# Preparing a projection pair's operands between the products of the pair before it, and sharing its input sums between two engines, in a two-layer hybrid backbone

## The chip, the core and the metric

The kernel runs on one core of a Trainium2 chip. The metric is the device time of one execution in microseconds (us), median over runs. The engines are TensorE (PE, with its weight loads as PEld), VectorE (DVE), ScalarE (ACT), GpSimd (POOL) and SyncE (SP), which here only issues DMAs.

## The reference, cut to what matters

Two layers work on 1024 latent and 256 context tokens of width 1024. A layer normalises and modulates its input to `h`, projects `h` with one matrix `w_in`, gives column groups of the result to four heads (neighbourhood attention, latent attention, a spatial gate, a short convolution), gates them, and projects the joined result back. Only layer 0 updates the context tokens.

```python
hx = modulate(rms_norm(x, norm_g), sh_x, sc_x)
hc = modulate(rms_norm(ctx, norm_g), sh_c, sc_c)
(a_q, a_k, a_v, a_g, b_cq, b_ckv, b_kr, b_g,
 c_u, c_v, c_g, d_b, d_c, d_h, d_g) = jnp.split(hx @ w_in, IN_SPLIT_POINTS, axis=-1)
...
x_new = x + g_x * merge_branches((out_a, out_b, out_c, out_d), (a_g, b_g, c_g, d_g), w_out)
```

The change concerns the product `hx @ w_in` for column groups of 256: `cg`, `dc`, `dh`, `db`, `dg`, `cq`, `ak`, `aq`, `bg`, `ag`.

## The kernel before

`h` is held transposed, as 8 tiles of 128 channels for each of two chunks of 512 latent tokens and one chunk of 256 context tokens, each tile as a high and a low part in a 32-bit matmul format (tag `g`). A plain block (`w_block`, `block_c`) loads 128 columns of weights (512 KB), casts them to a high part on ScalarE (line 362), subtracts it on GpSimd or VectorE for a low part (line 367), and makes three matmuls for each tile: high x high, high x low, low x high.

A pair (`proj2`) does 256 columns for both latent chunks with 7 products in place of 8, in Strassen's manner. `R` holds the right operands: three are tiles of `h` ("11", "21", "22"), four are differences ("1", "2", "3", "4"). For these, `right_parts(i)` adds the high and low parts of four tiles on GpSimd (line 709), `right_sums(i, t)` subtracts the sums on VectorE (line 716) and splits the differences into high and low parts; i runs over 0 to 3. For i of 2 and 3, "3" and "4" live in the tag `o`, whose four buffers hold the token weights of the `av` tiles until those are done. The left operands are four quarters `r` of the weights (four loads of 256 KB, line 736) and combinations of them (lines 740 to 743); `w_op` splits one into a buffer of the tags `wh`, `wl` and `wr` in turn, two buffers each. Operands 0 to 3 are made ahead of the products, 4, 5 and 6 after products 0, 2 and 3. A product is 12 matmuls of 512 columns.

Layer 0 (`half_paired`) makes the first groups as plain blocks, then `value_blocks` (ckv, ten context blocks, the sums, the `av` tiles), then the pairs cq, ak, aq, bg, and ag at the start of the attention stage. Layer 1 (`paired`) has ckv, ak's context blocks, the sums and the `av` tiles, then ten pairs from cg to ag. For bg and ag the tag `wr` is left out of the rotation; it holds two differences instead. Within ag `mla_load` brings attention's operands by DMA, into `g` buffers that the products give back. `kr_rotate` and `kr_transpose` prepare a rotary key between pairs, and `ckv_steps` sends a small power through GpSimd (line 218) on which transposes wait.

The order of instructions on each engine is written at build time by a planner with costs of its own (`schedule_with_timeline_sim=True`); the order of the program is its priority. It may place an instruction ahead of earlier ones that are not ready. `after(a, b)` fixes that a comes behind b on an engine; `pe.chain(True)` does so for all matmuls of a stretch. The tag `x` (20 buffers of 512) holds weights' quarters, sums, gate maps and more.

Of the kernel before, what the change touches and what calls it, by code (L numbers as in the profile page):

```python
# [11 lines left out]
F32R = mybir.dt.float32r  # L12
AF = mybir.ActivationFunctionType
ALU = mybir.AluOpType
# [35 lines left out]
V_NG, V_BM, V_QN, V_KV, V_LN, V_SC, V_FG = 0, 8, 32, 34, 35, 37, 43  # L50
# [46 lines left out]
def backbone(ctx: ExitStack, tc: tile.TileContext, a, yT, dbg=None):  # L97
# [85 lines left out]
    def f(ap):  # L183
        return ap.bitcast(F32)
# [49 lines left out]
    x = {}  # L234
# [191 lines left out]
    def layer(l, H):  # L426
# [263 lines left out]
                spill(scr["kr"][:, :, o:o + n].rearrange("h p n -> p h n"), f(st[64:128]))  # L690


        nop = [0]
        w_tags = ["wh", "wl", "wr"]

        def w_op(raw, lo_eng="pool"):
            t = T(w_tags[nop[0] % len(w_tags)], [2, 512], F32R)
            nop[0] += 1
            split(t[:, 0, :], t[:, 1, :], raw, lo_eng=lo_eng)
            return t.rearrange("p h (k n) -> p h k n", k=4)  # L700

        R = {}

        def right_parts(i):

            t = {}
            for k, (c, kc) in enumerate(((0, i), (1, i), (1, i + 4), (0, i + 4))):
                t[k] = T("x", [512])
                after(pool.tensor_tensor(t[k], f(H[c, kc][:, 0, :]), f(H[c, kc][:, 1, :]), ALU.add), last_split[0])  # L709
            R["11", i], R["21", i], R["22", i] = H[0, i], H[0, i + 4], H[1, i + 4]  # L710
            return t

# [13 lines left out]
                              skip_group_check=True)  # L726
                    n += 1

        def proj2(base, evac, mid={}, raw="x"):

            r = {}
            for j in range(2):
                t = T("st", [2, 512]) if raw == "st" else None
                for k in range(2):
                    r[j, k] = T("x", [512]) if t is None else t[:, k]
                    sp.dma_start(r[j, k], a["wtb"][l, BLOCKS.index(f"{base}{j}")][:, k * 512:(k + 1) * 512])
            qt = T("wr", [2, 512]) if "wr" not in w_tags else None
            q = [T("x", [512]) if qt is None else qt[:, k] for k in range(2)]
            a11, a12 = w_op(r[0, 0]), w_op(r[0, 1])
            dve.tensor_tensor(q[1], r[0, 0], r[1, 0], ALU.subtract)  # L740
            dve.tensor_tensor(r[1, 0], r[1, 0], r[1, 1], ALU.add)
            dve.tensor_tensor(q[0], r[1, 0], r[0, 0], ALU.subtract)
            dve.tensor_tensor(r[0, 1], r[0, 1], q[0], ALU.subtract)
            ops = {0: a11, 1: a12, 2: w_op(q[0], "dve"), 3: w_op(r[1, 0])}
            later = {0: (4, q[1], "dve"), 2: (5, r[0, 1], "dve"), 3: (6, r[1, 1], "pool")}
            x_, y_, z_ = PS("b", [512]), None, None

            def step(n, p, name, first=True):
                for fn in mid.get(n, []):
                    fn()  # L750
                product(p, ops[n], name, first)
                if n in later:
                    k, src, eng = later[n]
                    ops[k] = w_op(src, eng)

            def kept_copy(eng, p):
                t = T("tmp", [512])
                (eng.copy if eng is act else eng.tensor_copy)(t, p)
                return t

            step(0, x_, "11")
            m1 = kept_copy(act, x_)
            y_ = PS("b", [512])
            step(1, y_, "21")
            dve.tensor_tensor(m1, y_, m1, ALU.add)
            evac(0, m1, 0)
            step(2, x_, "2", False)
            u2 = kept_copy(act, x_)
            z_ = PS("b", [512])
            step(3, z_, "1")  # L770
            z5 = kept_copy(dve, z_)
            step(4, x_, "3", False)
            dve.tensor_tensor(z5, x_, z5, ALU.add)
            evac(1, z5, 1)
            step(5, z_, "22", False)
            dve.tensor_tensor(u2, z_, u2, ALU.add)
            evac(1, u2, 0)
            step(6, x_, "4", False)
            evac(0, x_, 1)

        def block_c(name, c, evac, **k):

# [39 lines left out]
                proj(f"db{j}", all_chunks, mulb)  # L822
                proj(f"dg{j}", all_chunks, lambda c, p: gate(c, p, fc))

        def value_blocks(ctx_first):

            wav = w_tok(a["wav"][l], 288, ("o", "o"), ("o", "o"))
            pe.chain(True)
            late = []

            def ckv_block(c, hi, lo):
                p = PS("b", [CHUNKS[c][1]])
                mm3(p, [(hi[:, kc, :], lo[:, kc, :], hap(c, kc, 0), hap(c, kc, 1)) for kc in range(KC)])
                late.append(ckv_steps(c, p))

            def on():
                for fn in [fns.pop(0) for fns in late if fns]:
                    fn()

            w = w_block(a["wtb"][l, BLOCKS.index("ckv0")])  # L840
            ckv_block(2, *w)
            ckv_block(1, *w)
            ckv_block(0, *w)
            for n, (name, fn) in enumerate(ctx_first):
                block_c(name, 2, fn, lo_eng=("dve", "pool")[n % 3 == 2])
# [12 lines left out]
            pe.chain(False)  # L858
            av_windows()

        def half_paired():
            first_groups()
            while fillers:
                fillers.pop(0)()
            park((4, 5, 6, 7))
            evacs = {"cq": cq_evac, "ak": k_evac, "aq": lambda c, p, j: q_evac(c, p, j, 0.125),
                     "bg": lambda c, p, j: act.activation(map_(2 + j, c), p, AF.Silu),
                     "ag": lambda c, p, j: act.activation(map_(j, c), p, AF.Silu)}
            value_blocks([(f"{n}{j}", lambda c, p, n=n, j=j: evacs[n](c, p, j)) for n in evacs for j in range(2)])
            proj2("cq", evacs["cq"])  # L870
            kr = kr_rotate()
            proj2("ak", k_evac)
            kr_transpose(*kr)
            proj2("aq", evacs["aq"])
            cq_stats()
            w_tags.remove("wr")
            proj2("bg", evacs["bg"])

        def paired():
            wav = w_tok(a["wav"][l], 288, ("o", "o"), ("o", "o"))  # L880
# [19 lines left out]
                fns.pop(0)()  # L900
            av_tile(8, wav)
            late[-1].pop()()
            parts.append(right_parts(1))
            for t in (9, 4):
                av_tile(t, wav)
            cv_gate(1)
# [7 lines left out]
                av_tile(t, wav)  # L914
            pe.chain(False)
            av_windows()
            proj2("cg", lambda c, p, j: gate(c, p, 4 + j))
            park((4, 5))
            proj2("dc", lambda c, p, j: act.copy(map_(6 + j, c), p))
            kr = kr_rotate()  # L920
            z = {}

            def conv_in(c, p, j):
                z[j, c] = T("x", [512])
                dve.tensor_tensor(z[j, c], p, map_(6 + j, c), ALU.mult)

            proj2("dh", conv_in)
            kr_transpose(*kr)
            for j in range(2):
                w = [v[:, V_SC + 3 * j + i:V_SC + 3 * j + i + 1] for i in range(3)]  # L930
                for c in range(2):
                    m = map_(6 + j, c)
                    act.activation(m, z[j, c], AF.Copy, scale=w[1])
                    for d, s_, k in ((m[:, 1:], z[j, c][:, :511], 0), (m[:, :511], z[j, c][:, 1:], 2),
                                     (m[:, 0:1], z[j, 0][:, 511:], 0) if c else (m[:, 511:], z[j, 1][:, 0:1], 2)):
                        dve.scalar_tensor_tensor(d, s_, w[k], d, ALU.mult, ALU.add)

            def mulb(c, p, j):
                m = map_(6 + j, c)
                dve.tensor_tensor(m, p, m, ALU.mult)  # L940

            proj2("db", mulb)
            proj2("dg", lambda c, p, j: gate(c, p, 6 + j))
            park((6, 7))
            proj2("cq", cq_evac)
            proj2("ak", k_evac)
            proj2("aq", lambda c, p, j: q_evac(c, p, j, 0.125))
            cq_stats()
            w_tags.remove("wr")
            proj2("bg", lambda c, p, j: act.activation(map_(2 + j, c), p, AF.Silu))  # L950

        ph = Phase("prj", ("o",))
        if last:
            paired()
        else:
            half_paired()


        ck, cq, up = {}, {}, {}
# [744 lines left out]
```

## Time and profile before

| | us |
|---|---|
| median of three runs | 1507.06 |
| the runs | 1506.96, 1512.91, 1507.06 |
| profiled execution | 1513.53 |
| its span, first to last instruction | 1511.7 |
| TensorE busy in it | 1402.0 (93%) |
| mean granted TensorE clock in it | 0.976 |

The granted clock is a share of the full 2.4 GHz. A busy TensorE is not TensorE at its peak: matmuls are pipelined, and at a lower clock the same matmuls are busy for longer.

### The profile page before, as it was taken

What the parts mean: (1) busy time and instruction counts of PE and PEld (TensorE: products, weight loads), DVE (VectorE), ACT (ScalarE), POOL (GpSimd) and SP (SyncE); (2) the same over time, 40 slices, a digit from 0 to 9 for tenths busy, and PEclk for the clock granted to TensorE, in tenths of its full rate; (3) what the DMA queues carried; (4) which work ended last, traced back from release to release, by engine and by line L of the source; (5) the groups of instructions that cost most, each with busy time, mean ns of one, the idle gap of its engine ahead of it and who ended that gap; (6) DMA issues with size and microseconds to landing.
All of it is one profiled execution on the core that took longest, in us unless ns stands there. A gap on an engine that the chain in (4) does not pass through costs nothing.

```text
span 1511.7 us, 23317 instructions
## 1 busy us (share of the span) xinstructions
PE 1402.0 (93%) x8784; PEld 1173.9 (78%) x8784; DVE 947.7 (63%) x2007; ACT 646.0 (43%) x1438; POOL 552.1 (37%) x441
## 2 busy tenths in 40 slices
PE   4999999896999999999999989799999899999997
PEld 3788888794777777778888889577787677778887
DVE  5867887365446776764555646747453677665564
ACT  5511111333344765654433422433343566655543
POOL 2154343266324000365712174734434001065651
PEclk9999999998899999999999999899999999999998
DMA  9414345514449000786333111340339403285331
GB/s 355 171 61 158 127 154 182 164 44 149 139 153 195 1 22 1 171 175 185 119 126 126 43 45 67 129 119 31 133 133 218 88 1 78 81 178 150 95 130 67
DMA packets 91312, 180.10 MB, mean 119 GB/s; under 512 B 9280, under 2 KB 35904, under 8 KB 91072
## 3 DMA queue, kind: packets, MB, share of 16 engines
q1 hardware_dynamic: 74176, 150.30, 30.5%
q0 software_dynamic: 15936, 27.27, 9.6%
q8 instruction: 69, 1.13, 0.3%
q10 hardware_dynamic: 1088, 1.05, 0.2%
q14 instruction: 43, 0.35, 0.1%
HBM read 144.77 MB, written 38.01 MB: 121 GB/s over the span
## 4 chain that ended last, share of the span: by engine, by line
PE 75%; DVE 6%; issue 5%; DMA 5%; POOL 4%; ACT 3%; SPq 1%; DVEq 0%; ACTq 0%; POOLq 0%
PE psb L173 59%; PE psv L173 7%; PE pst L176 7%; PE pst L173 1%; DMA x<-in_wtb 1%; DMA wr<-in_wtb 1%; POOL s L218 1%; POOL x L709 1%; DVE x L716 1%; DVE s L1106 1%; DMA g<-scr_cq 1%; POOL wl L367 1%; DVE pt L995 1%; ACT g L1253 1%; DMA wr<-in_wav 1%
## 5 line engine op out<-in xcount | busy, mean ns | idle before, releaser
L173 PE MATMUL psb<-g,wh 128*128 128x512 f32 (+1 forms) x1886 | 505.2, 370 | 26.2 <-ACT wh L362 22.0
L173 PEld LDWEIGHTS psb<-g,wh 128*128 128x128 f32 x1886 | 341.1, 193 | 92.7 <-ACT wh L362 24.6
L173 PE MATMUL psb<-g,wl 128*128 128x512 f32 (+1 forms) x1144 | 369.4, 375 | 11.9 <-ACT wl L362 7.3
L173 PEld LDWEIGHTS psb<-g,wl 128*128 128x128 f32 x1144 | 219.7, 193 | 55.2 <-ACT wl L362 9.4
L173 PE MATMUL psb<-g,st 128*128 128x512 f32 (+1 forms) x600 | 160.1, 383 | 10.3 <-ACT wl L1123 3.8
L1106 DVE TENSOR_REDUCE s<-psb 128x1 f32<-128x512 f32 (+1 forms) x200 | 117.3, 590 | 64.6 <-PE psb L173 62.7
L367 POOL TENSOR_TENSOR wl<-wr,wh 128x1024 fp32r<-128x1024 f32 (+1 forms) x38 | 92.9, 2445 | 137.3 <-ACT wh L362 136.1
L173 PE MATMUL psb<-g,g 128*128 128x256 f32 (+1 forms) x784 | 129.0, 305 | 1.8 <-ACT g L1123 0.8
L173 PEld LDWEIGHTS psb<-g,st 128*128 128x128 f32 x600 | 95.6, 192 | 34.8 <-issue 6.5
L173 PE MATMUL psv<-pt,g 128*64 128x256 f32 (+1 forms) x1312 | 119.4, 331 | 0.6 <-ACT pt L997 0.5
L997 ACT COPY pt<-pst 128x512 f32<-128x512 f32 x116 | 67.9, 585 | 111.5 <-PE pst L176 110.4
L173 PEld LDWEIGHTS psb<-g,g 128*128 128x128 f32 x784 | 105.3, 191 | 8.6 <-issue 2.9
L173 PEld LDWEIGHTS psv<-pt,g 128*64 128x64 f32 x1312 | 79.3, 137 | 32.5 <-issue 8.5
L173 PE MATMUL psb<-g,wr 128*128 128x512 f32 (+1 forms) x490 | 97.9, 346 | 5.1 <-ACT wr L362 2.6
L340 DVE CUSTOM_DVE_ANT_0 tmp<-g,x 128x512 f32<-128x512 f32 x112 | 92.5, 876 | 13.4 <-POOL x L490 11.2
L173 PEld LDWEIGHTS psb<-g,wr 128*128 128x128 f32 x490 | 77.5, 190 | 17.9 <-ACT wr L362 3.7
L176 PE MATMUL pst<-ident,g 128*128 128x128 f32 x448 | 79.1, 278 | 11.3 <-ACT g L1253 6.4
L364 POOL TENSOR_SCALAR wh<-wr 128x1024 fp32r<-128x1024 f32 x16 | 44.3, 2772 | 113.0 <-PE pst L176 53.2
L995 DVE COPY pt<-pst 128x512 f32<-128x512 f32 x116 | 79.1, 683 | 6.7 <-PE pst L176 6.1
L1439 DVE SCALAR_TENSOR_TENSOR x<-psb,modG,x 128x512 f32<-128x512 f32 (+1 forms) x48 | 29.5, 615 | 85.1 <-PE psb L173 45.6
L362 ACT CAST wh<-wr 128x1024 fp32r<-128x1024 f32 (+1 forms) x41 | 40.3, 986 | 91.0 <-PE psb L173 58.5
L176 PEld LDWEIGHTS pst<-ident,g 128*128 128x128 f32 x448 | 54.0, 140 | 28.0 <-ACT g L1253 8.3
(249 smaller groups left out, 2387.4 us busy)
## 6 DMA issues: line engine op xcount, KB each, us to landing
g<-in_wmod SPq DMA_DIRECT2D x48, 512.0 KB, 4.7
x<-in_wtb SPq DMA_DIRECT2D x60, 256.0 KB, 4.1
wr<-in_wtb SPq DMA_DIRECT2D x28, 512.0 KB, 4.1
wr<-in_wout SPq DMA_DIRECT2D x27, 512.0 KB, 3.8
st<-in_nab SPq DMA_DIRECT2D x24, 384.0 KB, 3.3
x<-in_xT SPq DMA_DIRECT2D x32, 256.0 KB, 5.8
g<-scr_q POOLq DMA_DIRECT2D x32, 256.0 KB, 7.2
x<-x SPq DMA_DIRECT2D x24, 256.0 KB, 2.5
```

The source lines that it names most:

```text
L173: return self._next(nc.tensor.matmul(*p, **k))
L176: return self._next(nc.tensor.transpose(*p, **k))
L218: pool.tensor_tensor(r0, v, mhalf[:, :n], ALU.pow)
L340: dve.tensor_tensor_reduce(junk, w[:, hf * 512:hf * 512 + 512], crow[cond, hf], 1.0, 0.0, ALU.mult, ALU.add, part[:, i, cond, hf:hf + 1])
L362: act.copy(hi, raw)
L364: pool.tensor_scalar(hi, raw, 1.0, None, ALU.mult)
L367: m = (pool if lo_eng == "pool" else dve).tensor_tensor(lo, raw, f(hi), ALU.subtract)
L709: after(pool.tensor_tensor(t[k], f(H[c, kc][:, 0, :]), f(H[c, kc][:, 1, :]), ALU.add), last_split[0])
L995: dve.tensor_copy(dst, src)
L997: act.copy(dst, src)
L1106: dve.reduce_max(st["mx"][:, i:i + 1], s_, AX.X)
L1439: dve.scalar_tensor_tensor(xa, p, mod[l]["G"][:, fb, cond:cond + 1], xa, ALU.mult, ALU.add)
```

## The change

`proj2` becomes a class `Pair` whose steps can be called one by one. `load` issues the four loads, `sums` makes three differences, `op` splits one operand (the fourth difference is made with operand 5), `prep` does the loads, the sums and operands 0 to 3. `run(nxt)` makes the seven products and, after products 1, 3, 4, 5 and 6, calls the next pair's `load`, `sums` and `op`. The first pair of each layer is prepared by `prep` ahead of the sums' `right_parts`; in layer 1 `right_parts(0)` and `(1)` stand together behind it. `right_parts` gives its first and third addition to VectorE. All pairs but ag use three operand tags; differences live in `x` buffers for all.

```diff
             for k, (c, kc) in enumerate(((0, i), (1, i), (1, i + 4), (0, i + 4))):
                 t[k] = T("x", [512])
-                after(pool.tensor_tensor(t[k], f(H[c, kc][:, 0, :]), f(H[c, kc][:, 1, :]), ALU.add), last_split[0])
+                m = (pool if k % 2 else dve).tensor_tensor(t[k], f(H[c, kc][:, 0, :]), f(H[c, kc][:, 1, :]), ALU.add)
+                after(m, last_split[0] if k % 2 else gated.get(1, gated[0]))
...
-        def proj2(base, evac, mid={}, raw="x"):
...
+        class Pair:
+
+            count = 0
+
+            def __init__(self, base, evac, mid={}, tags=("wh", "wl", "wr")):
+                self.base, self.evac, self.mid, self.tags, self.ops = base, evac, mid, tags, {}
+
+            def load(self):
+                self.r = r = {}
+                for j in range(2):
+                    for k in range(2):
+                        r[j, k] = T("x", [512])
+                        sp.dma_start(r[j, k], a["wtb"][l, BLOCKS.index(f"{self.base}{j}")][:, k * 512:(k + 1) * 512])
+
+            def sums(self):
+                r = self.r
+                self.q = q = [T("x", [512]) for _ in range(2)]
+                dve.tensor_tensor(q[1], r[0, 0], r[1, 0], ALU.subtract)
+                dve.tensor_tensor(r[1, 0], r[1, 0], r[1, 1], ALU.add)
+                dve.tensor_tensor(q[0], r[1, 0], r[0, 0], ALU.subtract)
+
+            def op(self, n):
+                r, q = self.r, self.q
+                if n == 5:
+                    dve.tensor_tensor(r[0, 1], r[0, 1], q[0], ALU.subtract)
+                src = (r[0, 0], r[0, 1], q[0], r[1, 0], q[1], r[0, 1], r[1, 1])[n]
+                t = T(self.tags[Pair.count % len(self.tags)], [2, 512], F32R)
+                Pair.count += 1
+                split(t[:, 0, :], t[:, 1, :], src, lo_eng="dve" if n in (2, 4, 5) else "pool")
+                self.ops[n] = t.rearrange("p h (k n) -> p h k n", k=4)
+
+            def prep(self):
+                self.load()
+                self.sums()
+                for n in range(4):
+                    self.op(n)
+
+            def run(self, nxt=None):
+                evac = self.evac
+                todo = {0: [lambda: self.op(4)], 2: [lambda: self.op(5)], 3: [lambda: self.op(6)]}
+                if nxt:
+                    todo[1] = [nxt.load]
+                    todo[3].append(nxt.sums)
+                    todo[4] = [lambda: nxt.op(0)]
+                    todo[5] = [lambda: nxt.op(1)]
+                    todo[6] = [lambda: nxt.op(2), lambda: nxt.op(3)]
...
+                def step(n, p, name, first=True):
+                    for fn in self.mid.get(n, []):
+                        fn()
+                    product(p, self.ops.pop(n), name, first)
+                    for fn in todo.get(n, []):
+                        fn()
...
-        def value_blocks(ctx_first):
+        def value_blocks(ctx_first, first):
...
             for t in (8, 9):
                 av_tile(t, wav)
+            first.prep()
             parts = [right_parts(0), right_parts(1)]
...
-            proj2("cq", evacs["cq"])
+            pairs = [Pair(n, evacs[n]) for n in ("cq", "ak", "aq", "bg")] + [ag_pair()]
...
+            pairs[0].run(pairs[1])
             kr = kr_rotate()
-            proj2("ak", k_evac)
+            pairs[1].run(pairs[2])
             kr_transpose(*kr)
-            proj2("aq", evacs["aq"])
+            pairs[2].run(pairs[3])
             cq_stats()
-            w_tags.remove("wr")
-            proj2("bg", evacs["bg"])
+            pairs[3].run(pairs[4])
...
+        def ag_pair():
+            return Pair("ag", lambda c, p, j: act.activation(map_(j, c), p, AF.Silu), {1: [lambda: mla_load()], 6: [lambda: mla_keys(0)]},
+                     ("wh", "wl"))
...
             late[-1].pop()()
-            parts.append(right_parts(1))
...
+            pairs["cg"].prep()
+            parts = [right_parts(0), right_parts(1)]
             for t in (9, 4):
                 av_tile(t, wav)
...
+            for name, nxt in zip(names, names[1:]):
+                pairs[name].run(pairs[nxt])
+                for fn in behind_pair.get(name, []):
+                    fn()
...
-        proj2("ag", lambda c, p, j: act.activation(map_(j, c), p, AF.Silu), {1: [mla_load], 6: [lambda: mla_keys(0)]})
+        ag_run.run()
```

`behind_pair` holds what stood between the pairs before (`park`, `kr_rotate`, `kr_transpose`, the convolution, `cq_stats`), at the same places.

## Rows read from the trace of the kernel before

**Rows 1.** Page, head and part 1: busy time, share of the span, instructions of each engine.

```profile
span 1511.7 us, 23317 instructions
...
PE 1402.0 (93%) x8784; PEld 1173.9 (78%) x8784; DVE 947.7 (63%) x2007; ACT 646.0 (43%) x1438; POOL 552.1 (37%) x441
```

**Rows 2.** Windows of layer 0; columns: length, busy time (instructions) of each engine, granted clock, DMA.

```profile
341.00:372.80 31.80, 22.74 (x84) 17.27 (x84) 20.14 (x21) 11.55 (x20) 18.11 (x14) 0.84 0.37 130
372.80:384.40 11.60, 4.16 (x13) 2.73 (x12) 3.91 (x6) 3.55 (x6) 9.62 (x18) 0.66 0.83 271
384.40:434.40 50.00, 49.99 (x216) 40.90 (x217) 27.48 (x41) 21.29 (x37) 14.57 (x10) 0.94 0.37 123
434.40:450.60 16.20, 13.72 (x57) 10.21 (x56) 4.96 (x12) 5.16 (x10) 2.66 (x4) 1.00 0.49 165
```

**Rows 3.** The same columns for stretches of layer 1.

```profile
899.20:904.00 4.80, 0.24 (x2) 0.00 (x0) 2.26 (x8) 0.60 (x1) 3.41 (x2) 0.81 0.00 0
948.50:1001.80 53.30, 42.40 (x168) 32.59 (x168) 30.85 (x33) 19.11 (x33) 34.65 (x35) 0.90 0.39 124
1001.80:1028.00 26.20, 22.41 (x100) 17.19 (x99) 17.28 (x25) 11.15 (x19) 6.54 (x6) 1.00 0.36 107
1028.00:1148.40 120.40, 119.67 (x516) 96.64 (x516) 70.53 (x96) 45.05 (x79) 43.94 (x30) 0.99 0.36 124
1148.40:1173.60 25.20, 23.36 (x94) 18.28 (x93) 10.53 (x17) 12.19 (x22) 18.12 (x22) 0.93 1.02 198
```

**Rows 4.** Timeline of layer 0, start of the first pair.

```profile
339.97 2.50 POOL L367 TENSOR_TENSOR o<-x,o 128x512 fp32r<-128x512 f32 x2 [9.82 <-ACT o L362]
...
342.43 5.39 POOL L709 TENSOR_TENSOR x<-g 128x512 f32<-128x512 f32 x4
...
347.78 1.71 POOL L367 TENSOR_TENSOR wh<-x,wh 128x512 fp32r<-128x512 f32 x1
...
350.75 5.46 PE L173 MATMUL psb<-g,wh 128*128 128x512 f32 x12 [7.26 <-ACT wh L362]
```

**Rows 5.** Timeline of layer 0, between the first and the second pair.

```profile
375.16 10.66 SPq L736 DMA_DIRECT2D x<-in_wtb  x10
...
376.63 3.33 POOL L675 TENSOR_TENSOR x<-tmp 128x128 f32<-128x128 f32 x8
...
378.24 1.22 PE L173 MATMUL psb<-g,wl 128*128 128x512 f32 x2 [5.43 <-ACT wl L362]
```

**Rows 6.** Timeline of layer 1, GpSimd's additions and TensorE behind them.

```profile
886.01 12.07 POOL L709 TENSOR_TENSOR x<-g 128x512 f32<-128x512 f32 x8
...
904.03 0.69 PE L176 MATMUL pst<-ident,s 128*128 128x128 f32 x2 [4.59 <-DVE s L223]
```

**Rows 7.** Lines 709 and 716, both layers: instructions, ns min/median/max, first and last start.

```profile
L709 POOL TENSOR_TENSOR x<-g x32: 1259/1292/2353, 302.4 to 954.8; 128x512 f32<-128x512 f32 x32
...
L716 DVE TENSOR_TENSOR x<-x,x x32: 675/1602/1790, 306.0 to 965.6; 128x512 f32<-128x512 f32 x32
```

**Rows 8.** Chain of work in order of time, end of layer 1's last pair.

```profile
1157.25 7.61 DMA g<-scr_ck
...
1165.37 10.54 DMA g<-scr_cq
```

**Rows 9.** Windows, layer 0's context blocks, columns as in rows 2.

```profile
268.50:308.80 40.30, 33.25 (x249) 31.82 (x249) 16.68 (x31) 14.36 (x25) 17.58 (x11) 0.92 0.51 164
```

**Rows 10.** Groups of instructions in the context blocks' stretch.

```profile
L362 ACT CAST wh<-wr 128x1024 fp32r<-128x1024 f32 x8 | 8.4, 1046 | 18.3 <-DMA wr<-in_wtb 9.5 <-PE psb L173 8.8
```

**Rows 11.** Page, part 6: DMA issues, KB each, us to landing.

```profile
wr<-in_wtb SPq DMA_DIRECT2D x28, 512.0 KB, 4.1
...
x<-in_wtb SPq DMA_DIRECT2D x60, 256.0 KB, 4.1
```

**Rows 12.** Timeline of SyncE's queue in layer 0, ahead of the context blocks.

```profile
213.91 0.33 SPq L395 DMA_DIRECT2D wr<-in_wav  x1
...
231.64 0.33 SPq L373 DMA_DIRECT2D wr<-in_wtb  x1
```

More of the change, by code (lines that the diff above doesn't have):

```diff
@@ L690, in kr_transpose @@
                 spill(scr["kr"][:, :, o:o + n].rearrange("h p n -> p h n"), f(st[64:128]))
[L693 to L700, printed above, removed]
         R = {}
@@ L727, in product @@
                     n += 1
-        def proj2(base, evac, mid={}, raw="x"):
[L731 to L779, printed above, removed]
@@ new lines, in layer, with kept_copy @@
+        class Pair:
[43 more added lines that the diff above has]
+                        fn()
+                def kept_copy(eng, p):
+                    t = T("tmp", [512])
+                    (eng.copy if eng is act else eng.tensor_copy)(t, p)
+                    return t
+                x_ = PS("b", [512])
+                step(0, x_, "11")
+                m1 = kept_copy(act, x_)
+                y_ = PS("b", [512])
+                step(1, y_, "21")
+                dve.tensor_tensor(m1, y_, m1, ALU.add)
+                evac(0, m1, 0)
+                step(2, x_, "2", False)
+                u2 = kept_copy(act, x_)
+                z_ = PS("b", [512])
+                step(3, z_, "1")
+                z5 = kept_copy(dve, z_)
+                step(4, x_, "3", False)
+                dve.tensor_tensor(z5, x_, z5, ALU.add)
+                evac(1, z5, 1)
+                step(5, z_, "22", False)
+                dve.tensor_tensor(u2, z_, u2, ALU.add)
+                evac(1, u2, 0)
+                step(6, x_, "4", False)
+                evac(0, x_, 1)
@@ L902, in paired @@
             late[-1].pop()()
-            parts.append(right_parts(1))
+            pairs = {"cg": Pair("cg", lambda c, p, j: gate(c, p, 4 + j)),
+                     "dc": Pair("dc", lambda c, p, j: act.copy(map_(6 + j, c), p)), "dh": Pair("dh", conv_in),
+                     "db": Pair("db", mulb), "dg": Pair("dg", lambda c, p, j: gate(c, p, 6 + j)),
+                     "cq": Pair("cq", cq_evac), "ak": Pair("ak", k_evac),
+                     "aq": Pair("aq", lambda c, p, j: q_evac(c, p, j, 0.125)),
+                     "bg": Pair("bg", lambda c, p, j: act.activation(map_(2 + j, c), p, AF.Silu)), "ag": ag_pair()}
+            pairs["cg"].prep()
+            parts = [right_parts(0), right_parts(1)]
             for t in (9, 4):
@@ L916, in paired @@
             av_windows()
[L917 to L950, printed above, removed]
+            names = list(pairs)
+            behind_pair = {"cg": [lambda: park((4, 5))], "dc": [lambda: kr.extend(kr_rotate())],
+                           "dh": [lambda: kr_transpose(*kr), conv], "dg": [lambda: park((6, 7))], "aq": [cq_stats]}
+            kr = []
+            for name, nxt in zip(names, names[1:]):
+                pairs[name].run(pairs[nxt])
+                for fn in behind_pair.get(name, []):
+                    fn()
+            return pairs["ag"]
         ph = Phase("prj", ("o",))
[L953 to L956, printed above, removed]
+        ag_run = paired() if last else half_paired()
         ck, cq, up = {}, {}, {}
```

19 lines of the change are left out of this document (18 added, 1 removed).

## The prediction

> **What bounds the kernel now.** I read part 1 of the page first. TensorE is busy for 1402 us of a span of 1511.7 us [rows 1], so only its idle time and its time at a low clock can be won. Next come the windows, which say where those lie in the two projection stages. In layer 0 TensorE works 22.74 of 31.80 us in the first pair, at a granted clock of 0.84, and 4.16 of 11.60 us between the first pair and the second, at 0.66 [rows 2]. From 384.4 on it is full. Layer 1 looks the same: 0.24 of 4.80 us before the last ckv steps, 42.40 of 53.30 us in the first two pairs, and then 119.67 of 120.40 us [rows 3]. The reader is to see that the middle pairs already run without gaps, so that this change can win only at the ends of the stages.
>
> Then the timeline shows what is waited for. At the first pair of layer 0 GpSimd splits the last "o" tiles, runs four additions of right_parts for 5.39 us, and only at 347.78 makes the low half of the pair's first operand; TensorE's next run of products starts at 350.75 after 7.26 us of waiting [rows 4]. Before the second pair SyncE issues its loads from 375.16, behind the spills of the first, and TensorE has waited 5.43 us when operand 0 comes [rows 5]. In layer 1 eight additions hold GpSimd for 12.07 us, and TensorE waits 4.59 us at 904.03 for a chain that needed GpSimd in that time [rows 6].
>
> **The price of a pair.** The covered stretch 1028.0 to 1148.4 holds 516 TensorE instructions in 120.40 us, 0.233 us each [rows 3]. A pair has 7 products of 12 matmuls, 84 x 0.233 = 19.6 us. The change adds and removes no matmul, so every stretch is priced as its TensorE instructions x 0.233.
>
> **Preparing ahead (Pair.prep, load, sums, op).** Layer 0 [rows 2]:
> - first pair, 31.80 - 19.6 = 12.2 us above price: its four loads, three sums and operands 0 to 3 move to before the av tiles that fill TensorE;
> - up to the second pair, 11.60 - 13 x 0.233 = 8.6 us: its loads move from behind the spills of cq to behind product 1;
> - 384.4 to 434.4, 50.00 - 216 x 0.233 = -0.3, so nothing;
> - bg to ag, 16.20 - 57 x 0.233 = 2.9 us: bg keeps the third operand tag and the differences leave it.
>
> That is 23.7 us. Layer 1 [rows 3]:
> - first two pairs, 53.30 - 168 x 0.233 = 14.2 us;
> - third pair, 26.20 - 100 x 0.233 = 2.9 us: the fourth pair's loads no longer stand behind kr's spills;
> - 1028.0 to 1148.4, 0;
> - last pair, 25.20 - 94 x 0.233 = 3.3 us.
>
> That is 20.4 us, and 44.1 us for both layers, if nothing is late next.
>
> **Halved additions.** Moving two of four additions to VectorE takes 2 x 1.29 = 2.6 us off GpSimd per call [rows 7]. Behind the last "o" split this leaves 2.6 instead of 5.39 us before GpSimd is free [rows 4], so the differences for products 2, 3, 4 and 6 come about when TensorE wants them, 5.6 us after the start (two products). This is part of the 12.2 and 14.2 us and not counted again. In layer 1 the additions also move behind the prepared operands, out of the way of the chain at 904.03: another 4.80 - 2 x 0.233 = 4.3 us [rows 3, 6]. The ceiling is 44.1 + 4.3 = 48.4 us.
>
> VectorE pays: an addition or subtraction of this shape takes it 0.675 us at best and 1.60 in the median, while GpSimd's holds at 1.29 [rows 7]. I read this as VectorE being held while GpSimd works. Eight calls x 2 additions x 0.675 to 1.60 us is 11 to 26 us of VectorE time, nearly all of it while av tiles occupy TensorE. Cover gone, only the two calls for the last index would show, at up to 3.2 us each.
>
> The Trainium skill (SBUF — State Buffer, "SBUF: two separate sides") speaks against this edit: it says that GpSimd and a VectorE instruction with two SBUF inputs exclude each other from one port pair for a whole instruction. By that rule four additions take 2 x (1.29 + 0.675) = 3.9 us instead of about 3.2 in parallel. The sum would be some 1.4 us worse; the rows agree for VectorE, whose median is drawn out, and not for GpSimd.
>
> **What is late next.** I take off:
> - First pairs: VectorE is busy 20.14 us and GpSimd 18.11 us in the 31.80 us of layer 0's first pair [rows 2]. Of these some 4 us of sums and low halves leave VectorE for earlier, and about as much comes in for the next pair. 20 us of VectorE work in 19.6 us cannot fit without gaps. Nothing to 5 us per layer; I take 3, so 6.
> - kr_rotate: its eight copies alone take GpSimd 3.33 us [rows 5], in a gap that vanishes. They now stand between low halves of operands. Nothing to 3.3 us per layer; I take 1 in all, since an operand is due two products after its cast.
> - The prepared work itself: no row shows loads, casts and sums of a pair among context blocks or av tiles. From below, nothing: that stretch's DMA share is 0.51 and TensorE idles 7 of 40.3 us anyway [rows 9]. From above, one load, 4.1 us [rows 11], on the path in each layer, 8.2 us. I take 2, nearer to nothing, because four loads lie among free queue time.
> - The end: ag's keys and queries arrive by transfers of 7.61 and 10.54 us, one after the other [rows 8], and the first can start only when the first products have given their buffers back. 2.8 + 7.6 + 10.5 = 20.9 us from the pair's start stands against 19.6 us of products, so 1 to 2 us come back. I take 1.
>
> The sum of these is 10 us (0 to 23.5: 10, 3.3, 8.2 and 2). 48.4 - 10 = 38.4 us.
>
> The sum was made against the profiled execution, 1513.5 us (span 1511.7 and 1.8 around it); that gives 1475. It is 6.5 us above the median of the runs, 1507.1, and I found no stretch to put that on. I take the saving over unchanged: 1507.1 - 38.4 = 1468.7, say **1469 us**.
>
> **The clock.** The first two windows of rows 2 were granted 0.84 and 0.66, a mixture of 2.4 GHz and of 1.2 GHz after TensorE's waits; pricing them at 0.233 us already counts that back. The Trainium skill (TensorE: Matmul & The Clock Gate, "What's actually happening") calls the low state the default, released by activity; the rows agree, and no extra term follows.
>
> **Rivals.**
> 1. *VectorE and GpSimd become the bound of the first pairs.* For: 20.14 and 18.11 us busy in layer 0's first pair, 30.85 and 34.65 us in layer 1's first two [rows 2, 3]. Against: part of it moves ahead. If the first pairs kept half of what they have above price, (12.2 + 14.2)/2 = 13.2 us, and the other three costs were at their upper ends, 13.5, the saving is 48.4 - 26.7 = 21.7: about 1485 us. Chance 0.18.
> 2. *Written order changes little.* The order on each engine is a planner's, and before the change it already issued ten loads in a row, two pairs ahead [rows 5]. It may place the new program's loads as late as before. Then only the additions count: 4.3 us, and 2.6 + 2.6 us at the starts, about 1497 us. Against: the late loads stood behind spills that come first in the program, and this order is now reversed. Chance 0.08.
> 3. *Slower: the prepared operands sit in the context blocks' buffers.* Operands 0 to 3 need four of the six wh, wl and wr buffers, from prep to the pair. If they got them before layer 0's last context blocks had theirs, these would run one at a time: load 4.1, cast 1.05 and products 33.25/10 = 3.3 us are at least 8.4 instead of 40.3/10 = 4.0 us a block [rows 9 to 11], 4.4 us more. With all ten it is 44 us, which eats the whole gain of 38; with these costs on top, 1513 us. It decides from nine blocks on. Against: the loads of wav, written between two other users of wr, went out between them, at 213.91 and before the 231.64 of the next weight block [rows 12], so a tag's buffers are handed out in program order, and prep stands behind the last context block. Chance 0.05.
>
> **How the numbers follow.** My forecast (saving 28 to 50 us, 1457 to 1479) has 0.69, the rivals 0.18, 0.08 and 0.05. The range 1453 to 1490 takes in the forecast with the costs at nothing, 1507.1 - 48.4 = 1459 and some room below for gaps that I priced as covered, and most of rival 1; it leaves out rivals 2 and 3 and the tails, about 0.18. About 0.5%, 7.5 us, is what a measurement of this kernel can tell from no change. The forecast and the first two rivals lie below that, but for a little of the second: faster 0.92, same 0.03, slower 0.05.
>
> **What would show it.** Right: TensorE in layer 0 goes from the last av tile into 24 matmuls of products 0 and 1 without a wait; the first load of ak leaves SyncE before the first spill of cq; no wait near 904 in layer 1; the windows of the first pairs shrink from 31.8 to some 22 us and from 53.3 to some 43, at a clock near 1. Wrong: new waits of TensorE on low halves by VectorE or GpSimd in the first pairs (rival 1), loads still behind spills (rival 2), context blocks longer than the 40.3 us of rows 9 (rival 3), or a longer wait on the last transfers.

## The result and the profile after

The changed kernel takes **1470.65 us** (median of four runs, 1469.06 to 1471.41) against 1507.19 us before (four runs), a ratio of 0.9747 with a 95% interval of 0.9722 to 0.9772 (the two medians alone give 0.9758). The forecast was 1469, the range 1453 to 1490. The total was right by luck: two of its terms were wrong, in opposite directions.

**What both texts ahead left out.** In layer 1 the changed program still calls `right_parts(0)` behind `cv_gate(0)`, and calls it again behind `prep`. The first call's four sums are never read. So there are 36 additions, not 32; the prediction counted eight calls.

The page of the changed kernel, head and part 1, beside [rows 1]:

```profile
span 1467.3 us, 23300 instructions
...
PE 1380.6 (94%) x8784; PEld 1161.1 (79%) x8784; DVE 960.9 (65%) x2025; ACT 643.0 (44%) x1438; POOL 538.3 (37%) x427
```

TensorE has the same 8784 matmuls in a span 44.4 us shorter. Cut at events of TensorE, the profiled executions divide as follows (differences of start and end times in the timelines, us; for the experiments too, which come below). "to av end" is the span's start to layer 0's last av tile, "pairs 0" from there to the last product of ag, "to gate" from there to the first matmul of layer 1's `cv_gate(0)`, "ckv, av" from there to layer 1's last av tile, "pairs 1" to its last product of ag, "rest" to the end.

| kernel | to av end | pairs 0 | to gate | ckv, av | pairs 1 | rest |
|---|---|---|---|---|---|---|
| before | 341.0 | 132.2 | 432.9 | 42.2 | 225.2 | 338.1 |
| after | 339.1 | 108.5 | 427.6 | 55.4 | 202.9 | 333.8 |
| one call | 341.0 | 106.9 | 428.0 | 52.3 | 202.9 | 334.8 |
| all on GpSimd | 336.2 | 110.9 | 428.1 | 55.5 | 207.8 | 339.2 |
| first pairs late | 338.9 | 111.8 | 428.7 | 51.0 | 211.4 | 334.5 |
| nothing between products | 339.2 | 121.9 | 430.1 | 56.2 | 215.3 | 335.2 |
| halving alone | 340.6 | 129.9 | 429.1 | 47.9 | 221.3 | 335.9 |
| VectorE's behind ckv | 341.7 | 108.4 | 427.6 | 48.1 | 202.8 | 334.2 |
| both behind ckv | 339.4 | 106.9 | 428.2 | 48.7 | 202.8 | 335.5 |
| GpSimd alone, behind ckv | 337.5 | 112.9 | 427.6 | 47.7 | 207.1 | 334.8 |
| tiles ahead | 338.1 | 108.4 | 427.6 | 45.3 | 202.5 | 333.7 |
| tiles ahead, both behind | 341.1 | 106.8 | 427.6 | 41.0 | 208.5 | 334.1 |

Before to after: 1.9 + 23.7 + 5.3 - 13.2 + 22.3 + 4.3 = 44.3 us. The medians lie 36.5 us apart, because the profiled execution of before was 6.3 us above its median and that of after 1.6 us below.

Layer 0's pairs, in windows with the columns of [rows 2]:

```profile
339.10:358.70 19.60, 16.28 (x67) 12.36 (x67) 14.22 (x19) 8.62 (x17) 13.42 (x10) 0.98 0.63 215
358.70:378.30 19.60, 19.32 (x79) 15.37 (x78) 10.50 (x12) 7.85 (x14) 14.41 (x21) 0.93 0.50 164
378.30:397.90 19.60, 19.60 (x95) 16.14 (x95) 12.39 (x19) 7.80 (x14) 3.88 (x3) 1.00 0.62 209
397.90:447.60 49.70, 49.70 (x225) 40.64 (x224) 27.18 (x43) 22.99 (x41) 27.22 (x30) 1.00 0.88 226
```

A window of 19.6 us is as long as the price of a pair, and the first one holds 67 of the first pair's 84 matmuls. The whole pair goes from 339.10 to 363.92, where the second pair's first matmul starts: 24.82 us, with TensorE busy for 21.50, VectorE for 17.24 and GpSimd for 15.82 us, at a clock of 0.93. For the same 84 matmuls the first line of [rows 2] has 31.80 us, 22.74, 20.14, 18.11 and 0.84. The timeline there, beside [rows 4]:

```profile
338.93 2.94 PE L173 MATMUL psb<-g,wh 128*128 128x512 f32 x12
...
341.71 2.96 PE L173 MATMUL psb<-g,wl 128*128 128x512 f32 x12
342.48 2.54 POOL L700 TENSOR_TENSOR x<-g 128x512 f32<-128x512 f32 x2
...
351.37 2.37 PE L173 MATMUL psb<-g,wl 128*128 128x512 f32 x9 [1.16 <-POOL wl L367]
...
354.81 0.69 DVE L740 TENSOR_TENSOR x<-x,x 128x512 f32<-128x512 f32 x1
355.59 0.62 ACT L362 CAST wh<-x 128x512 fp32r<-128x512 f32 x1 [4.74 <-DVE x L740]
356.11 0.58 ACT L777 COPY tmp<-psb 128x512 f32<-128x512 f32 x1
...
356.74 2.02 PE L173 MATMUL psb<-g,wl 128*128 128x512 f32 x6 [2.16 <-ACT tmp L777]
```

Products 0 and 1 start behind the last av tile without a wait, where 7.26 us were waited before; GpSimd's two additions (line 700 is now that of `right_parts`) still run beside product 1. One wait of 1.16 us and two on an eviction, a copy out of a matmul buffer (2.4 us together), are what is left in these pairs. The longer of the two, 2.16 us, comes from VectorE: ScalarE's copy (line 777) stands behind a cast that waited 4.74 us for VectorE's sums of the second pair (line 740). SyncE's queue shows why the second pair no longer waits, beside [rows 5]:

```profile
339.77 0.89 SPq L733 DMA_DIRECT2D x<-in_wtb  x2
...
341.24 0.88 SPq L733 DMA_DIRECT2D x<-in_wtb  x2
...
354.20 13.59 SPq L560 DMA_DIRECT2D scr_cq<-st  x3
```

ak's four loads leave at 339.8 to 342.1, ahead of the first spill of cq at 354.20; before, the first left at 373.81 and the next from 375.16, behind the spills.

In layer 1 TensorE's waits from the spatial gate to ag's end are these (line waited for, releaser: us in total, times, longest):

```profile
PE pst L176 <- DVE s L223: 13.1, 1, 13.1
PE psb L173 <- ACT tmp L777: 1.6, 3, 0.8
PE psb L173 <- ACT g L362: 0.9, 1, 0.9
```

The first of them is new. The timeline around it:

```profile
884.07 0.15 DVE L598 TENSOR_SCALAR s<-pst 128x4 f32<-128x4 f32 x1
...
884.34 1.46 POOL L218 TENSOR_TENSOR s<-s,mhalf 128x4 f32<-128x4 f32 x1
...
887.77 1.74 DVE L740 TENSOR_TENSOR x<-x,x 128x512 f32<-128x512 f32 x1
888.93 6.78 POOL L700 TENSOR_TENSOR x<-g 128x512 f32<-128x512 f32 x4
889.44 1.75 DVE L700 TENSOR_TENSOR x<-g 128x512 f32<-128x512 f32 x1
891.11 1.22 DVE L220 SCALAR_TENSOR_TENSOR s<-s,s 128x4 f32<-128x4 f32 x1
892.25 4.01 DVE L700 TENSOR_TENSOR x<-g 128x512 f32<-128x512 f32 x3
...
897.56 0.15 DVE L223 SCALAR_TENSOR_TENSOR s<-s,s 128x4 f32<-128x4 f32 x1
...
897.85 1.08 PE L176 MATMUL pst<-ident,s 128*128 128x128 f32 x4 [13.11 <-DVE s L223]
```

The last ckv step's power on GpSimd is done at 885.80. Its three small scalings on VectorE (lines 220 to 223) end at 897.71, 11.9 us later, because sums of the pair's quarters, low halves and four additions stand between them. The four transposes wait for them, and av tiles stand behind the transposes. The windows (columns as above) show the clock there:

```profile
880.00:885.00 5.00, 4.74 (x38) 4.51 (x37) 5.00 (x8) 2.17 (x5) 5.00 (x4) 1.00 0.45 153
885.00:890.00 5.00, 0.00 (x0) 0.00 (x0) 5.00 (x5) 1.87 (x4) 5.00 (x4) 0.69 0.41 149
890.00:895.00 5.00, 0.00 (x0) 0.00 (x0) 5.00 (x5) 0.22 (x1) 5.00 (x4) 0.50 0.00 0
895.00:900.00 5.00, 2.15 (x10) 2.18 (x11) 4.02 (x8) 0.88 (x2) 0.71 (x1) 0.50 0.00 0
```

TensorE idles for 13 us and comes back at 0.50, 1.2 GHz: its four transposes take 1.08 us, against 0.60 us for four like them at 880.06.

### The profile page after: what moved, and what is told of

The parts are those of the page before. It is cut to its first block, busy times and chain, and to the rows that moved or that the text cites. A ratio compares the mean times of both kernels' runs of the same rounds, so it can differ in the third digit from the quotient of the medians.

```text
span 1467.3 us, 23300 instructions
## 1 busy us (share of the span) xinstructions
PE 1380.6 (94%) x8784; PEld 1161.1 (79%) x8784; DVE 960.9 (65%) x2025; ACT 643.0 (44%) x1438; POOL 538.3 (37%) x427
## 5 line engine op out<-in xcount | busy, mean ns | idle before, releaser
L173 PE MATMUL psb<-g,wh 128*128 128x512 f32 (+1 forms) x1862 | 489.4, 363 | 4.3 <-ACT x L502 1.4
L173 PEld LDWEIGHTS psb<-g,wh 128*128 128x128 f32 x1862 | 330.7, 189 | 65.2 <-ACT x L502 1.9
L173 PE MATMUL psb<-g,wl 128*128 128x512 f32 (+1 forms) x1114 | 356.3, 369 | 5.7 <-ACT tmp L777 3.1
L173 PEld LDWEIGHTS psb<-g,wl 128*128 128x128 f32 x1114 | 210.1, 189 | 44.7 <-ACT tmp L777 4.4
L173 PE MATMUL psb<-g,wr 128*128 128x512 f32 (+1 forms) x544 | 110.4, 348 | 1.1 <-ACT g L362 0.9
L173 PEld LDWEIGHTS psb<-g,wr 128*128 128x128 f32 x544 | 87.7, 189 | 15.1 <-ACT g L362 1.3
L364 POOL TENSOR_SCALAR wh<-wr 128x1024 fp32r<-128x1024 f32 x16 | 44.3, 2772 | 113.0 <-PE pst L176 52.9
```

The source lines that it names most:

```text
L173: return self._next(nc.tensor.matmul(*p, **k))
L364: pool.tensor_scalar(hi, raw, 1.0, None, ALU.mult)
```

## The experiments

The theory at the start was that VectorE's share of the additions holds the scalings of the last ckv step. The rival was that the planner puts the additions, on whichever engine, and the prepared work ahead of that step. A second question was how the gain divides among preparing the first pairs early, preparing between products, and halving. All edits are to the changed kernel unless said otherwise. The times of before in the three sets of runs were 1508.77, 1510.19 and 1510.79 us; ratios are to before in the same set. Beside the changed kernel before took 1507.19 us, so up to 3.6 us of a difference between medians of two sets can be that of the sets.

**One call.** The unread first call is taken out.

```diff
             cv_gate(0)
-            parts = [right_parts(0)]
```

> Changed kernel (1470.7 us) without the first of the two calls of right_parts(0) in layer 1, whose four sums nothing reads. Theory A (VectorE's queue: additions and prepared sums stand inside the ckv scaling chain, and TensorE waits 13.1 us for it near 885 us): two VectorE additions of about 1.75 us and two of GpSimd leave that stretch, the wait falls by 3 to 5 us, 1466 to 1468. Theory B (the wait is set by GpSimd's power, lines 218, behind its own additions): GpSimd had 2.5 us of them ahead of the power, the wait falls by at most 2.5 us, 1468 to 1471.

Measured: 1466.40 us, 0.9718 (0.9695 to 0.9741). The wait fell from 13.1 to 8.7 us, as in the first case. The time is 4.3 us lower than after's, but the two intervals overlap; it is the wait that shows the gain. In the timeline of this run both engines are in the way:

```profile
884.80 4.52 DVE L700 TENSOR_TENSOR x<-g 128x512 f32<-128x512 f32 x3
...
885.39 6.71 POOL L700 TENSOR_TENSOR x<-g 128x512 f32<-128x512 f32 x4
...
889.57 0.14 DVE L598 TENSOR_SCALAR s<-pst 128x4 f32<-128x4 f32 x1
...
892.07 1.46 POOL L218 TENSOR_TENSOR s<-s,mhalf 128x4 f32<-128x4 f32 x1
```

Three additions on VectorE stand ahead of the instruction that makes the power's input (line 598), which ends at 889.71. Four on GpSimd then hold the power itself until 892.07. The scalings follow it at once, at 893.56.

**All on GpSimd.** The additions are not halved; the unread call stays.

```diff
-                m = (pool if k % 2 else dve).tensor_tensor(t[k], ...)
-                after(m, last_split[0] if k % 2 else gated.get(1, gated[0]))
+                m = pool.tensor_tensor(t[k], ...)
+                after(m, last_split[0])
```

> Changed kernel with all additions of right_parts on GpSimd again, all behind the last split (the doubled call stays). Theory A: the four VectorE additions that stand between the steps of the ckv chain go, the wait of 13.1 us in layer 1 falls to 3 to 8 us and the half clock behind it goes too; the starts of the first pairs lose at most 2.6 us a layer: 1462 to 1470. Theory B (halving is what lets the pairs start in time): both first pairs start late again by 5 to 10 us each, 1478 to 1490.

Measured: 1478.18 us, 0.9804 (0.9779 to 0.9829), 7.5 us above after. The wait at the last ckv stays, 11.9 us, now behind GpSimd:

```profile
884.80 10.24 POOL L700 TENSOR_TENSOR x<-g 128x512 f32<-128x512 f32 x8
895.00 1.02 POOL L218 TENSOR_TENSOR s<-s,mhalf 128x4 f32<-128x4 f32 x1
```

The theory falls as it was put: its time and its shorter wait are both missed. The wait is the work of the order: whichever engine has the additions, the planner puts them ahead of the last ckv step. The time is at the lower edge of the second case's, but the first pairs do not lose 5 to 10 us each: pairs 0 lose 2.4 us and pairs 1 4.9. Another 5.4 us lie in the "rest" of this execution, and no run shows their cause.

**First pairs late.** Each layer's first pair is prepared right before its products.

```diff
-            first.prep()
...
+            pairs[0].prep()
             pairs[0].run(pairs[1])
...
-            pairs["cg"].prep()
...
+            pairs["cg"].prep()
             for name, nxt in zip(names, names[1:]):
```

> Changed kernel with the first pair of each layer prepared right before its products and not ahead of the additions; the later pairs as in the change. Theory A: the first pair of layer 0 loses most of the 12.2 us that it had above price before, layer 1's some 8 to 10 us; in the ckv stretch of layer 1 the prepared sums leave VectorE's queue and the wait falls by some 5 us: 1480 to 1488. Theory B (halved additions carry the starts): at most 5 us lost at the starts, 1466 to 1474.

Measured: 1478.35 us, 0.9801 (0.9782 to 0.9820), 7.7 us above after: pairs 0 are 3.3 us longer, pairs 1 8.5, and the ckv stretch is 4.4 us shorter. Its wait is still 8.2 us with no prepared work in it, so the additions alone make one of that size. The time lies below the first case's range and above the second's: layer 0's pairs do not lose most of the 12.2 us. The edit undoes the early preparation there only in part, because the planner still sends two of the pair's four loads at 336.60, before the last av tile ends at 338.90.

**Nothing between products.** Each later pair is prepared at the start of its own products.

```diff
-                if nxt:
-                    todo[1] = [nxt.load]
-                    todo[3].append(nxt.sums)
-                    todo[4] = [lambda: nxt.op(0)]
-                    todo[5] = [lambda: nxt.op(1)]
-                    todo[6] = [lambda: nxt.op(2), lambda: nxt.op(3)]
+                if not self.ops:
+                    self.prep()
```

> Changed kernel with prep and halved additions kept, but each later pair prepared at the start of its own run, behind all of the pair before it, as the old program had it. Theory A (written order counts where loads stood behind spills): the second pair of layer 0 loses some 8 us, layer 1's second and third pair some 3 to 6 us, bg to ag up to 3 us a layer: 1484 to 1492. Rival (the planner hoists anyway): within 3 us of the changed kernel, 1468 to 1474.

Measured: 1499.55 us, 0.9944 (0.9925 to 0.9964), 28.9 us above after and more than the expected 1484 to 1492: pairs 0 lose 13.4 us, pairs 1 12.4. SyncE's queue shows the loads back among the spills, and TensorE a wait like that of 5.43 us in [rows 5]:

```profile
362.74 0.44 SPq L560 DMA_DIRECT2D scr_cq<-st  x1
363.28 11.24 SPq L733 DMA_DIRECT2D x<-in_wtb  x11
```

```profile
366.18 1.22 PE L173 MATMUL psb<-g,wl 128*128 128x512 f32 x2 [5.30 <-ACT wl L362]
```

So the place of the steps in the program decides; the planner did not move them up by itself (rival 2 of the prediction). This part is the largest. How much of it is the loads' and how much the sums' and casts' was not taken apart.

**Halving alone.** The kernel before with the first lines of the change's diff and nothing else.

```diff
-                after(pool.tensor_tensor(t[k], ...), last_split[0])
+                m = (pool if k % 2 else dve).tensor_tensor(t[k], ...)
+                after(m, last_split[0] if k % 2 else gated.get(1, gated[0]))
```

> The kernel before with one part of the change alone: the first and third additions of each call on VectorE. Theory (the halving only shortens GpSimd's queue at the first pairs and at the last ckv's power): two calls' 2.6 us in layer 0 and up to 4.6 us of the wait near 904 in layer 1, so 3 to 10 us, 1497 to 1505 us. Rival (VectorE's additions hold the scaling of the last ckv as in the changed kernel): the wait near 904 grows beyond 4.6 us and the time is 1505 to 1512.

Measured: 1504.61 us, 0.9971 (0.9954 to 0.9987), 4.4 us. Pairs 0 gain 2.3 us and pairs 1 3.9. The 4.59 us wait ahead of the gate goes and one of 4.9 comes behind it: even here the wait is moved, not removed. The time is at the top of the first case's range; the wait, a little longer than 4.6 us, is the second case's.

**VectorE's additions behind the last ckv step** (one call; layer 1 alone).

```diff
-                dve.tensor_tensor(st[:, 1, :], raw, f(st[:, 0, :]), ALU.subtract)
+                ckv_end[0] = dve.tensor_tensor(st[:, 1, :], raw, f(st[:, 0, :]), ALU.subtract)
...
-                after(m, last_split[0] if k % 2 else gated.get(1, gated[0]))
+                after(m, last_split[0] if k % 2 else gated[1] if 1 in gated else ckv_end[0])
```

> One call of right_parts(0), and in layer 1 only VectorE's additions ordered behind the last ckv step; GpSimd's stay where the planner puts them. If GpSimd's four additions ahead of the power are the link that holds the transposes, a wait of 4 to 9 us stays near 890 and the time is 1460 to 1466 us; if VectorE's additions alone did it, the wait goes and the time is 1453 to 1459.

Measured: 1462.25 us, 0.9685 (0.9661 to 0.9709), with a wait of 5.2 us. Time and wait are in the first case's range, but its mechanism is not there: bound on one engine only, the planner left GpSimd's additions behind the power too (power 887.36, additions from 888.78).

**Both behind the last ckv step.** As before this, and GpSimd's additions behind the power.

```diff
-        pool.tensor_tensor(r0, v, mhalf[:, :n], ALU.pow)
+        last_pow[0] = pool.tensor_tensor(r0, v, mhalf[:, :n], ALU.pow)
...
+                ckv_pow[0] = last_pow[0]
...
+                if k % 2 and last:
+                    after(m, ckv_pow[0])
```

> One call of right_parts(0), and in layer 1 the additions stand by an explicit order behind the last ckv step's own work: VectorE's behind its last VectorE instruction, GpSimd's behind its power. Order theory (the planner puts the additions ahead of the last ckv's power and scaling, on whichever engine they are): TensorE's wait of 8.7 us near 890 and the half clock behind it go, the stretch from the spatial gate to the last av tile falls from 52.3 to 42 to 45 us, and the time from 1466 to 1453 to 1459 us. Rival (the wait comes from the prepared operands' sums and splits, or from the transposes themselves): a wait of 5 us or more stays and the time is 1462 to 1468. Rival (the additions are late next): the wait goes, but TensorE waits as long for differences in layer 1's first pair, 1464 to 1470.

Measured: 1462.79 us, 0.9691 (0.9670 to 0.9712). A wait of 5.25 us stays: the first rival's case. Against the run with one call the intervals of the times overlap, and it is the wait, 8.70 us there, that shows the gain. The timeline (the power is line 220 here, the additions 706, low halves 369):

```profile
882.12 0.15 DVE L602 TENSOR_SCALAR s<-pst 128x4 f32<-128x4 f32 x1
...
882.39 1.75 POOL L369 TENSOR_TENSOR wh<-x,wh 128x512 fp32r<-128x512 f32 x1
...
884.10 1.45 POOL L220 TENSOR_TENSOR s<-s,mhalf 128x4 f32<-128x4 f32 x1
...
885.52 4.91 POOL L706 TENSOR_TENSOR x<-g 128x512 f32<-128x512 f32 x4
885.58 1.22 DVE L222 SCALAR_TENSOR_TENSOR s<-s,s 128x4 f32<-128x4 f32 x1 [0.90 <-POOL s L220]
886.83 1.18 DVE L223 TENSOR_TENSOR s<-s,s 128x4 f32<-128x4 f32 x1
888.05 1.19 DVE L225 SCALAR_TENSOR_TENSOR s<-s,s 128x4 f32<-128x4 f32 x1
...
889.38 1.09 PE L176 MATMUL pst<-ident,s 128*128 128x128 f32 x4 [5.25 <-DVE tmp L574]
```

Two things are left. A low half of the prepared pair holds GpSimd until 884.1, 1.8 us after the power's input was there. And each of the three scalings takes 1.2 us while GpSimd adds; with GpSimd idle in the run with one call they took 0.16 us each. The chain itself, 7.1 us from 882.12 to the last scaling's end, is longer than the one av tile, 3.4 us, that TensorE has in that time.

**GpSimd alone, behind the last ckv step.** The same order with the additions not halved: the lines of "all on GpSimd" with `after(m, ckv_pow[0])` in layer 1.

> As the run with both kinds of additions ordered behind the last ckv step, but with all of the additions on GpSimd. It separates what halving them is worth from what their place costs. If halving is worth its 7 to 8 us by itself, this is 1460 to 1467 us, with waits of TensorE on differences in the first pairs and on the transfer of the queries at the end. If the worth of halving seen before was only its share of the wait at the last ckv, this is within 3 us of the run with the additions halved.

Measured: 1468.99 us, 0.9739 (0.9708 to 0.9769), 6.2 us above the run with them halved. The ckv stretch is as short, so halving's worth is not its share of that wait: pairs 0 lose 6.0 us, pairs 1 4.3. The expected time, 1460 to 1467, was a little low, and the wait for the queries at the end that was expected with it is not there. In layer 0's first pair GpSimd is held by the additions until 348.42, 11.0 us after the pair's first matmul; in the halved run its two were done at 345.26, 6.0 us after it:

```profile
342.95 5.47 POOL L706 TENSOR_TENSOR x<-g 128x512 f32<-128x512 f32 x4
...
348.38 1.72 POOL L369 TENSOR_TENSOR wh<-x,wh 128x512 fp32r<-128x512 f32 x1
...
350.71 0.72 PE L173 MATMUL psb<-g,wh 128*128 128x512 f32 x2 [1.46 <-DVE g L369]
```

**Tiles ahead.** One call, additions where the planner wants them; TensorE gets two more av tiles ahead of the transposes.

```diff
-            av_tile(8, wav)
+            for t in (8, 9, 4):
+                av_tile(t, wav)
             late[-1].pop()()
...
             parts = [right_parts(0), right_parts(1)]
-            for t in (9, 4):
-                av_tile(t, wav)
             cv_gate(1)
```

> One call of right_parts(0), the additions wherever the planner puts them, and in layer 1 the av tiles 9 and 4 stand ahead of the last ckv step's transposes in TensorE's order, and so ahead of the preparation too. Order theory (what costs the time is only that TensorE has one av tile of 3.4 us to do while the power and the scaling pass GpSimd and VectorE): two more tiles of 3.4 to 4 us cover most of the wait of 8.7 us, 1 to 2 us of it are left, the half clock behind it goes, and the time falls from 1466 to 1455 to 1460 us. Rival (the chain is late in proportion, because the planner puts still more of the prepared work ahead of it): a wait of 5 us or more stays and the time is 1463 to 1468 us.

Measured: **1458.13 us**, 0.9643 (0.9619 to 0.9667), the lowest median of the study and 8.3 us below the run with one call. The chain is as long as there (the power at 890.43 behind four additions of 6.84 us), but TensorE waits 2.44 us of it, not 8.70, and the stretch falls from 52.3 to 45.3 us. The half clock behind the wait was expected to go and has not gone: the granted clock is 0.61 from 892.6 to 897.0.

```profile
883.63 6.84 POOL L700 TENSOR_TENSOR x<-g 128x512 f32<-128x512 f32 x4
890.43 1.47 POOL L218 TENSOR_TENSOR s<-s,mhalf 128x4 f32<-128x4 f32 x1
...
892.64 0.73 PE L176 MATMUL pst<-ident,s 128*128 128x128 f32 x4 [2.44 <-DVE tmp L572]
```

**Tiles ahead, both behind.** The edits of "both behind the last ckv step" and of "tiles ahead" together.

> The same order of tiles with the additions also ordered behind the last ckv step as in the earlier run of that (wait of 5.3 us left there, 1462.8 us). Order theory: two tiles of 3.4 to 4 us cover the 5.3 us whole, the stretch from the spatial gate to the last av tile falls to 41 to 44 us, and the time is 1454 to 1459 us. Rival: additions and differences that start later delay layer 1's first pair, which then waits 2 us or more, and the time is 1460 us or more.

Measured: 1461.35 us, 0.9660 (0.9634 to 0.9686). The wait at the transposes is gone and the stretch is 41.0 us, but pairs 1 grow from 202.5 to 208.5: the rival's case. The waits now lie in the first pair, 2.3 us on a cast of an operand and 1.4 us on differences, with a granted clock of 0.73 from 926.0 to 936.4:

```profile
PE psb L173 <- ACT wl L364: 2.3, 1, 2.3
...
PE psb L173 <- ACT g L364: 1.4, 2, 1.2
```

Additions held back behind the ckv step come late to the pair: TensorE starts it at 916.3, 2.9 us earlier than with the tiles ahead alone, but GpSimd's last two additions end at 925.1, 0.85 us later. Hiding the chain was here at least as good as also hurrying it at their expense: the medians lie 3.2 us apart, and the intervals overlap.

## Why the prediction was right in sum and wrong in two terms

- **Layer 0's pairs**, ceiling 23.7: measured 23.7, and the equality is luck, as the point on the price shows. The marks named for it are there: 24 matmuls without a wait, ak's loads ahead of cq's spills.
- **Layer 1's pairs**, ceiling 20.4: measured 22.3.
- **The price, 0.233 us an instruction: too high.** The first pair of each layer took longer than its price, and the other pairs less (windows of the changed kernel, cut at each pair's first matmul, us):

| pairs | measured | TensorE instructions | at 0.233 us | difference |
|---|---|---|---|---|
| layer 0, first | 24.82 | 84 | 19.6 | +5.2 |
| layer 0, other four | 83.68 | 385 | 89.7 | -6.0 |
| layer 1, first | 21.65 | 84 | 19.6 | +2.1 |
| layer 1, other nine | 181.25 | 797 | 185.7 | -4.5 |

- **Taken off, 10 us: the first pairs' 6 were about right, the rest was not.** The first pairs paid 7.3 us, 5.2 of it in layer 0, with a wait of 1.16 us for GpSimd and one of 2.16 us behind VectorE's sums, and a clock of 0.93. That is rival 1's mechanism in small. No wait falls on `kr_rotate`. The context blocks are not longer, against the 2 us for prepared work and against rival 3: the 40.3 us of [rows 9] now hold 251 of TensorE's instructions, 249 before. That "to av end" is 1.9 us shorter tells nothing, since it lies between 336.2 and 341.7 in all runs. The last transfers are no longer waited for: 1.8 us on the queries before, nothing after, where the forecast lost 1 us; what else of the 4.3 us in "rest" belongs to the change stays open, since the runs of other variants lie between 333.7 and 339.2.
- **The ckv stretch, 4.3 us: wrong in sign.** The step that failed is "the additions also move behind the prepared operands, out of the way of the chain at 904.03". The 4.59 us wait of [rows 6] went (5.3 us to the gate), but program order is only the planner's priority: additions, operand sums and low halves were put ahead of the next ckv step's power and scalings, and a wait of 13.1 us came one step later, +13.2 us. The sum of both is +7.9 us instead of -4.3. The experiments share the wait out: 4.4 us go with the unread call (13.11 to 8.70), 3.45 with the place of the other additions (8.70 to 5.25), and the rest is a chain that one av tile cannot cover.
- **Halving**, taken as part of the pairs' gain: shown, 4.4 us alone and 6.2 us with the additions out of the ckv step's way, near the 2.6 us for each layer's first pair. The reading that GpSimd's addition holds at 1.29 us was wrong, as the last section shows.
- **Small slips of the working.** The upper ends of what was taken off count `kr_rotate`'s 3.3 us once, though it is said to be per layer; with both layers' rival 1 comes to some 1489 us, still within the range. TensorE is full from 384.4 to 434.4 only, not to the end of [rows 2]. The eight "copies" of `kr_rotate` in [rows 5] are additions.

So the errors cancelled. The forecast for the pairs was 44.1 - 7 (first pairs and `kr_rotate`) = 37.1 us, and 46.0 came. In the profiled executions 38.4 + 8.9 (pairs) + 3.9 (to av end, with the 2 taken off for prepared work) + 5.3 (rest, with the 1 for the end) - 12.2 (ckv stretch) = 44.3 us; 7.9 of these are the distance of the two profiled executions from their medians, which leaves 36.4 of the 36.5. The saving was rightly taken off the median, but not all of the 44.3 can then be the change's.

Of the 36.5 us the preparation between products carries most (28.9 us when undone), the early first pairs 7.7 and halving 7.5, all between medians of two sets. These overlap and are not a sum.

## What to carry to other kernels

Work that is moved off the critical path lands in some other stage: look there for short chains that cross two engines (a power, a scaling, a transpose), and count what TensorE has to do while they run, because the planner here put long independent work into them, eight additions of 10.24 us in one run. Give TensorE cover for such a chain before you reorder the engines it crosses; with that cover in place, holding the long work back as well only moved the wait to its consumer. After a refactoring count the instructions of each changed line: 18 and 18 additions where 16 and 16 were due showed a call whose result nobody read.

## What the runs showed of the hardware

Additions slow each other on both engines. The groups of line 700 in the changed kernel (count, then ns min, median and max):

```profile
L700 DVE TENSOR_TENSOR x<-g x18: 678/1772/1786, 309.4 to 930.2; 128x512 f32<-128x512 f32 x18
L700 POOL TENSOR_TENSOR x<-g x18: 1275/1721/1777, 310.6 to 934.5; 128x512 f32<-128x512 f32 x18
```

GpSimd's median is 1.72 us beside VectorE's additions; with all 36 on GpSimd it is 1.315. In the run with one call two and two, side by side from 919.08 to 923.71, took 4.63 us; four on GpSimd alone, with one of VectorE's differences beside them, took 5.47. The gain of sharing is thus small where both run at once; the 6.2 us are rather won where they do not, as in layer 0's first pair, but were not taken apart further. The prediction had read the exclusion as VectorE's alone. The Trainium skill (SBUF — State Buffer, "SBUF: two separate sides") had it for both sides; these rows agree with it in kind. The prediction's estimate of 3.9 us for four is below the 4.63 measured.

The same effect is, in proportion, dearest on the smallest instructions seen here: a 128x4 scaling with two inputs takes 0.16 us with GpSimd idle and 1.2 us while GpSimd adds, so three of them in a row cost 3.6 us instead of 0.5, on a chain that TensorE waits for.
